# A norm's column sum in another product's stream, an earlier scan, and a state part whose output goes by groups in alternating halves

## The chip, the core and the metric

The kernel runs on one core of a Trainium2 chip. The metric is the device time of one execution in microseconds (us). Engines: TensorE (PE in the profile, its weight loads PEld), VectorE (DVE), ScalarE (ACT), GpSimd (POOL) and SyncE (SP), which issues most transfers.

## The reference, cut to what matters

Two blocks follow one another on 512 tokens of 2048 channels. The change touches the first: the norm of x, the projection by `w_in`, and of its four quarters the one that goes through a state-space mixer.

```python
hn = rmsnorm(h, norm_gain[i])           # x * rsqrt(mean(x*x) + eps) * gain, per token
proj = hn @ w_in[i]                      # (512, 2048) @ (2048, 4096)
pool_in, pool_gate, ssm_in, ssm_gate = four quarters of proj, 1024 channels each
...
# ssm_mixer: 64 groups of 16 channels, 64 complex states each
bu = einsum('blgc,gnc->blgn', u, bb)     # complex
s[t] = ab * s[t-1] + bu[t]               # per group and state, complex
y = Re(einsum('blgn,gcn->blgc', s, c)) + d_skip * u
g = gelu(y)
hg = g @ w_glu
out = hg[..., :1024] * sigmoid(hg[..., 1024:])
```

## The kernel before

**The stream of weights.** All large products run on TensorE in single precision, each operand split into a high and a low part, so that one tile product is three matmuls. Weights come in pieces of two k-tiles (128 rows of the contraction by 512 columns each): SyncE loads a piece (`raw`), ScalarE casts it to the high part (`whi`, L250), VectorE subtracts for the low part (`wlo`, L182). Loads run six pieces ahead, the splitting three. `gemm` (L288 on) does twelve matmuls of 128x512 per k-tile and then calls `tick()`.

**What sets the order.** Everything else on TensorE is put between k-tiles: `side(steps, ticks, least)` (L117) registers a list of steps, and each `tick()` runs the next ones, one per tick or at the rate that `least` and the length give; `None` is an empty step. TensorE's instructions stand in the order in which the program writes them; the order on the other engines is set by a scheduler when the program is built. Temporary tiles come from pools: `t4` with 30 buffers, `t2` with 8, PSUM with five banks for the large products (`mm`) and three for the rest (`aux`).

**The norm of x.** The first two products are linear in x, so x goes in unscaled, and the factor per token is multiplied in afterwards. It comes from the generator `norm_x`: the column sum of the squares (`colsum`, L897: four matmuls into `norm_x`), then `rsq` on VectorE (fourteen small operations, `rsv`, `rsy`, `rst`), then `rows` (L345: four transposes that spread the factor over the partitions) and its copy `r1row`. `put` multiplies a result tile by `r1row` and stores it to `ud` in DRAM. In `blocks` (L1589) the column sum is at tick 13 of the first product, `rsq` behind it at high priority, and `rows` at the first tick of the second product, with the first four `put` behind.

**The state part.** One side list begins with the second product and goes on through the gates' six products. It builds tables (`ssm_tables`, products of 128x1024 named `bb`, `bbt`), then for each half h of the 64 groups and each j of four: `pw` (powers of the transition, 128x1024 on VectorE), `kk` (eight matmuls), two `wb` steps (transposes), `uu` (the load of U from `ud` on SyncE's queue), and `xx` (eight matmuls, whose result ScalarE copies into the states `XS`). After a table `kd` is stored to DRAM, the scan runs on VectorE: 63 recurrences of four small operations each (`sc`, `XS`), three per tick. Then the output: `prep(j, h)` loads T (from `kd`, on GpSimd's queue), computes O (three products), and has ScalarE copy the shifted states into `sx` (L641, two copies); `mm(j, h, g4)` (L653, L654) does eight matmuls with weights of 64 columns and 128 moving columns, into the 64 partitions of PSUM that belong to half h, and ScalarE copies them to `yv`; `fin` transposes and applies the gelu.

**Beside it.** `K.ada(0, 5)` is a second side list with the modulation vector of the second block, spread over the 96 ticks of the gates: loads `wa` on SyncE's queue, products on VectorE (L191) and tiny matmuls `fin` (L946).

Of the kernel before, what the change touches and what calls it, by code (L numbers as in the profile page):

```python
# [16 lines left out]
P = 128  # L17
# [22 lines left out]
class Kernel:  # L40
# [504 lines left out]
    def ssm_in_steps(self, h):  # L545

        nc = self.nc
# [43 lines left out]
        steps = [lambda: pw(0)]  # L591
        for j in range(4):
            steps += [lambda j=j: (kk(j), wb(j, 0)), lambda j=j: wb(j, 1), lambda j=j: uu(j)]
            if j < 3:
                steps.append(lambda j=j: pw(j + 1))
            steps.append(lambda j=j: xx(j))
        if h == 1:
            def kd():
                self.kd = self.dram("kd", [2 * P - 16, 1024])
                z = self.t4("z", [P, 1024])  # L600
                nc.gpsimd.memset(z, 0.0)
                nc.gpsimd.dma_start(self.kd[P:, :], z[:P - 16, :])
                nc.gpsimd.dma_start(self.kd[:P, :], self.ksb.rearrange("p g c -> p (g c)"))
            steps.append(kd)
# [15 lines left out]
    def ssm_out_steps(self):  # L620
# [4 lines left out]
        def init():  # L625
            self.d2 = self.c_table(1)
            st["T"] = [self.t4("T", [P, 8, 8, 16]) for _ in range(2)]

        def prep(j, h):
            gs = slice(h * 32 + j * 8, h * 32 + j * 8 + 8)  # L630
            T = st["T"][h]
            kd = self.kd[:P, gs.start * 16:gs.stop * 16]
# [3 lines left out]
            o = st["o", j, h] = self.t4("O", [P, 8, 8, 16])  # L636
            self.powers(o, 0, gs, self.d1, self.d2)
            sx = st["sx", j, h] = self.t2("sx", [P, 8, 64])
            nc.vector.memset(sx[:, :, 0], 0.0)
            for r in range(2):  # L640
                nc.scalar.copy(sx[r * 64:r * 64 + 64, :, 1:64],  # L641
                               self.XS[h * 64:h * 64 + 64, 0:63, r, j * 8:j * 8 + 8].rearrange("p k g -> p g k"))
            if h == 0:
                st["yv", j] = self.t4("yv", [P, 8, P])

        def mm(j, h, g4):
            hp = slice(h * 64, h * 64 + 64)
            T, o, sx = st["T"][h], st["o", j, h], st["sx", j, h]
            ps = self.aux("mm")
            for gg in range(4):  # L650
                g = g4 * 4 + gg
                out = ps[hp, gg * P:(gg + 1) * P]
                nc.tensor.matmul(out, self.U[j][:, h, g, :], T[:, :, g, :], start=True, stop=False)  # L653
                nc.tensor.matmul(out, sx[:, g, :], o[:, g].rearrange("p i c -> p (i c)"), start=False, stop=True)  # L654
            nc.scalar.copy(st["yv", j][hp, :, g4 * 64:(g4 + 1) * 64].rearrange("p i (g c) -> p g i c", g=4),
                           ps[hp, :].rearrange("p (g i c) -> p g i c", g=4, i=8))
# [16 lines left out]
        steps = [init, lambda: prep(0, 0)]  # L673
        for j in range(4):
            for h in range(2):
                n = 2 * j + h + 1
                if n < 8:
                    steps.append(lambda n=n: prep(n // 2, n % 2))
                steps += [lambda j=j, h=h: mm(j, h, 0), lambda j=j, h=h: mm(j, h, 1)]
            if j > 0:  # L680
                steps += [lambda j=j: fin(j - 1, 0), lambda j=j: fin(j - 1, 1)]
# [907 lines left out]
def blocks(K, a, dbg):  # L1589
# [16 lines left out]
    K.side([None] * 13 + [lambda: next(norm, None)], 14)  # L1606
# [4 lines left out]
    with K.tc.high_priority():  # L1611
        next(norm, None)
    K.finish(s)
    out, halve = K.ssm_out_steps()
    K.side([lambda: next(norm, None)] + [lambda i=i: put(i, first[i], first[i]) for i in range(4)], 5)
    ssm = K.side([None] + K.steps(K.ssm_tables(), 5) + [None] * 4 + K.ssm_in_steps(0) + K.ssm_in_steps(1)
                 + out[:1] + K.ssm_scan_steps() + out[1:], 111)
# [6 lines left out]
    ada = K.side(K.ada(0, 5), 96, 0)  # L1624
# [34 lines left out]
```

## Time and profile before

| | us |
|---|---|
| median of 3 runs (lowest to highest) | 3242.53 (3242.39 to 3245.29) |
| the profiled execution | 3245.36 |
| its span | 3243.6 |
| its mean granted clock of TensorE | 0.991 |

The profile is of one execution. Its span is the time between its first and its last instruction; 1.8 us lie around it. Rows are told by line of the program, engine, operation and tile names (out<-in). A single-precision matmul that isn't split stands in the trace as two records. A row's duration can reach a little over the start of the next row on its engine, since operations are pipelined; where a cost is a share of a sequence it is taken from start to next start. `PEclk` is the clock granted to TensorE, as a share of full speed (2.4 GHz); 0.50 is its lower level, 1.2 GHz.

### The profile page before, as it was taken

The page shows a single profiled execution, that of the slowest core. Times are in us where ns is not written, and L with a number is a line of the kernel's source. Part 1 is how long each engine was busy: PE and PEld are TensorE (multiplying, and loading weights), DVE is VectorE, ACT ScalarE, POOL GpSimd, SP SyncE. Part 2 cuts the span into 40 slices and gives each one's busy share as a digit, 9 for nine tenths or more (in the row PEclk, how much of TensorE's full clock was granted, in tenths as well). Part 3 has the DMA queues.
Part 4 walks back from the last instruction along what each step waited for, and adds up shares of the span by engine and source line. Part 5 has one row for each costly group of instructions (what it writes and reads, how often), then busy time and mean ns, then how long its engine had stood idle before and what let it go on. Part 6 is the DMA issues. An engine that isn't in the chain of part 4 may idle for free.

```text
span 3243.6 us, 50768 instructions
## 1 busy us (share of the span) xinstructions
PE 3161.7 (97%) x18812; PEld 2783.9 (86%) x18812; DVE 2378.8 (73%) x4659; ACT 1332.7 (41%) x2004; POOL 62.1 (2%) x114
## 2 busy tenths in 40 slices
PE   7998999999999999999999899999999999999998
PEld 6887787888899777778779799999999999888887
DVE  8569556876888677776755977888888888864445
ACT  6332453223356454443534553333434334333433
POOL 0000000000000000000000000000000000000000
PEclk9999999999999999999999999999999999999999
DMA  6555444865657444353425563444444444964664
GB/s 193 179 181 188 150 150 152 272 188 166 204 173 256 160 133 153 121 172 121 133 78 169 172 218 104 116 120 118 118 118 118 118 118 146 359 211 154 194 198 160
DMA packets 403865, 531.35 MB, mean 164 GB/s; under 512 B 42544, under 2 KB 225968, under 8 KB 403616
## 3 DMA queue, kind: packets, MB, share of 16 engines
q1 hardware_dynamic: 393408, 503.03, 49.4%
q0 software_dynamic: 5856, 17.11, 1.8%
q10 hardware_dynamic: 4352, 7.96, 0.7%
q8 instruction: 147, 2.41, 0.3%
q14 instruction: 102, 0.84, 0.1%
HBM read 491.34 MB, written 36.63 MB: 163 GB/s over the span
## 4 chain that ended last, share of the span: by engine, by line
PE 86%; DVE 9%; DMA 2%; issue 1%; ACT 1%; SPq 0%; DVEq 0%; ACTq 0%
PE mm L303 37%; PE mm L1390 17%; PE mm L1500 14%; PE p L1390 7%; PE mm L301 5%; DVE wlo L182 2%; PE probs L1070 2%; DMA wa<-in_w_ada_dram 1%; PE mix L1118 1%; DVE sc L182 1%; DVE ada L191 1%; PE turn L1110 1%; PE mm L653 1%; DVE acc L182 0%; PE mm L654 0%
## 5 line engine op out<-in xcount | busy, mean ns | idle before, releaser
L182 DVE TENSOR_TENSOR wlo<-raw,whi 128x1024 fp32r<-128x1024 f32 (+1 forms) x607 | 751.8, 1240 | 508.7 <-ACT whi L250 434.7
L250 ACT CAST whi<-raw 128x1024 fp32r<-128x1024 f32 (+1 forms) x455 | 491.9, 1082 | 890.3 <-PE mm L303 501.4
L303 PE MATMUL mm<-H,whi 128*128 128x512 f32 (+1 forms) x2048 | 514.5, 343 | 2.2 <-ACT pp L863 2.2
L1500 PE MATMUL mm<-whi,u 128*128 128x512 f32 x1344 | 414.7, 390 | 0.0
L303 PEld LDWEIGHTS mm<-H,whi 128*128 128x128 f32 x2048 | 347.9, 191 | 49.3 <-issue 9.8
L303 PE MATMUL mm<-H,wlo 128*128 128x512 f32 (+1 forms) x1024 | 346.2, 338 | 1.5 <-DVE wlo L182 1.5
L303 PE MATMUL mm<-X,whi 128*128 128x512 f32 x1024 | 325.9, 400 | 7.0 <-ACT whi L250 6.6
L268 ACT CAST whi<-raw 128x1024 fp32r<-128x1024 f32 x152 | 159.7, 1051 | 400.8 <-issue 232.4
L303 PE MATMUL mm<-M,whi 128*128 128x256 f32 (+1 forms) x1408 | 312.9, 318 | 4.6 <-ACT u L194 1.9
L1500 PEld LDWEIGHTS mm<-whi,u 128*128 128x128 f32 x1344 | 251.6, 188 | 52.1
L191 DVE SCALAR_TENSOR_TENSOR ada<-wa,siluc,ada 128x512 f32<-128x512 f32 x360 | 269.1, 747 | 36.2 <-DMA wa<-in_w_ada_dram 31.4
L1500 PE MATMUL mm<-wlo,u 128*128 128x512 f32 x672 | 261.5, 389 | 0.0
L303 PEld LDWEIGHTS mm<-M,whi 128*128 128x128 f32 x1408 | 235.3, 194 | 20.9 <-ACT u L194 2.1
L303 PEld LDWEIGHTS mm<-X,whi 128*128 128x128 f32 x1024 | 190.8, 191 | 48.1 <-ACT whi L250 6.6
L1390 PE MATMUL mm<-s,thi 128*128 128x256 f32 x1216 | 232.0, 283 | 0.0
L1390 PE MATMUL mm<-M,whi 128*128 128x256 f32 x1216 | 231.9, 283 | 0.0
L303 PE MATMUL mm<-M,wlo 128*128 128x256 f32 (+1 forms) x704 | 222.3, 316 | 5.0 <-DVE wlo L182 5.0
L303 PEld LDWEIGHTS mm<-H,wlo 128*128 128x128 f32 x1024 | 195.3, 191 | 23.1 <-DVE wlo L182 1.7
L303 PE MATMUL mm<-X,wlo 128*128 128x512 f32 x512 | 202.1, 395 | 0.5 <-DVE wlo L182 0.5
L1390 PEld LDWEIGHTS mm<-M,whi 128*128 128x128 f32 x1216 | 189.8, 192 | 0.1
L1390 PEld LDWEIGHTS mm<-s,thi 128*128 128x128 f32 x1216 | 189.7, 192 | 0.0
L1390 PE MATMUL mm<-M,wlo 128*128 128x256 f32 x608 | 172.1, 283 | 0.0
(377 smaller groups left out, 5806.5 us busy)
## 6 DMA issues: line engine op xcount, KB each, us to landing
wa<-in_w_ada_dram SPq DMA_DIRECT2D x192, 512.0 KB, 6.0
raw<-in_w_in_dram SPq DMA_DIRECT2D x111, 512.0 KB, 3.8
raw<-in_w_down_dram SPq DMA_DIRECT2D x88, 512.0 KB, 4.2
raw<-in_w_out_dram SPq DMA_DIRECT2D x80, 512.0 KB, 3.9
ur<-us SPq DMA_DIRECT2D x140, 256.0 KB, 4.6
raw<-in_w_in_dram SPq DMA_DIRECT2D x130, 256.0 KB, 3.1
raw<-in_w_ple_gate_dram SPq DMA_DIRECT2D x48, 512.0 KB, 3.9
raw<-in_w_gate_dram SPq DMA_DIRECT2D x152, 128.0 KB, 2.1
```

The costliest lines, as they stand in the source:

```text
L182: self.nc.vector.tensor_tensor(o, x, y, op=op)
L191: self.nc.vector.scalar_tensor_tensor(o, x, s, y, op0=op0, op1=op1)
L250: nc.scalar.copy(h, r)
L268: nc.scalar.copy(hv, v)
L301: nc.tensor.matmul(ps[i], x[k][:, xi, c], wt[:, a, :], **fl)
L303: nc.tensor.matmul(ps[i][:, cs], wt[:, a, c], x[k][:, xi, cs], **fl)
L653: nc.tensor.matmul(out, self.U[j][:, h, g, :], T[:, :, g, :], start=True, stop=False)
L1070: nc.tensor.matmul(ps[:, :n], q[:, i * P:n], k[:, :n], start=True, stop=True)
L1110: nc.tensor.transpose(pt[:, b * P:(b + 1) * P], p[:, b * P:(b + 1) * P], self.ident)
L1118: nc.tensor.matmul(po[:, :P], pT[:, b * P:(b + 1) * P], v(b, h), start=(b == 0), stop=(b == i))
L1390: nc.tensor.matmul(ps[j][:, s], wt[:, s, slot], self.C[k][j][xi], start=(k == 0 and s == 0 and i == 0), stop=(k == 7 and s == 1 and i == 2))
L1500: nc.tensor.matmul(ps[b], u[a][:, xi, b * P:(b + 1) * P], wt[:, a, :], start=(n == a == j == 0), stop=(n == NU - 1 and a == 1 and j == 2))
```

## The change

1. The column sum of the norm moves out of the first product into the second, to its second tick; `rsq` follows two ticks later, without high priority; `rows` comes at the seventh tick, and the four `put` at the eighth to eleventh.
2. The load of U is issued in the step of `kk` and the first `wb`; a step per j and half falls away, eight in all. The scan comes eight ticks earlier, and nine empty ticks are put behind it.
3. `kd` is stored by eight transfers, with its columns in the order j, group of four, half, instead of one.
4. The output goes by groups of four with both halves in one tile: `prep(j, g4)` loads a T for it (from the `t4` pool; before there were two fixed T tiles) and computes an O by six products of half the size; the `sx` copies for both halves are made at `g4 == 0`. `mm(j, g4)` does sixteen matmuls, whose halves alternate, into all 128 partitions of PSUM; eight such steps stand in place of sixteen of eight matmuls, and one copy to `yv` in place of two.
5. `K.ada(0, 5)` has 28 empty steps behind its first 24.

```diff
--- before.py
+++ after.py
@@ -590,7 +590,7 @@
 
         steps = [lambda: pw(0)]
         for j in range(4):
-            steps += [lambda j=j: (kk(j), wb(j, 0)), lambda j=j: wb(j, 1), lambda j=j: uu(j)]
+            steps += [lambda j=j: (uu(j), kk(j), wb(j, 0)), lambda j=j: wb(j, 1)]
             if j < 3:
                 steps.append(lambda j=j: pw(j + 1))
             steps.append(lambda j=j: xx(j))
@@ -600,7 +600,12 @@
                 z = self.t4("z", [P, 1024])
                 nc.gpsimd.memset(z, 0.0)
                 nc.gpsimd.dma_start(self.kd[P:, :], z[:P - 16, :])
-                nc.gpsimd.dma_start(self.kd[:P, :], self.ksb.rearrange("p g c -> p (g c)"))
+
+                for n in range(8):
+                    j, g4 = divmod(n, 2)
+                    nc.gpsimd.dma_start(self.kd[:P, n * P:(n + 1) * P].rearrange("p (h n) -> p h n", h=2),
+                                        self.ksb.rearrange("p (h g) c -> p h (g c)", h=2)
+                                        [:, :, (j * 8 + g4 * 4) * 16:(j * 8 + g4 * 4 + 4) * 16])
             steps.append(kd)
         return steps
 
@@ -624,36 +629,42 @@
 
         def init():
             self.d2 = self.c_table(1)
-            st["T"] = [self.t4("T", [P, 8, 8, 16]) for _ in range(2)]
-
-        def prep(j, h):
-            gs = slice(h * 32 + j * 8, h * 32 + j * 8 + 8)
-            T = st["T"][h]
-            kd = self.kd[:P, gs.start * 16:gs.stop * 16]
+
+        def prep(j, g4):
+
+            T = st["T", j, g4] = self.t4("T", [P, 8, 8, 16])
+            n = 2 * j + g4
+            kd = self.kd[:P, n * P:(n + 1) * P]
 
             nc.gpsimd.dma_start(T.rearrange("p i g c -> p i (g c)"),
                                 bass.AP(tensor=kd.tensor, offset=kd.offset, ap=[[1024, P], [16 * 1024, 8], [1, P]]))
-            o = st["o", j, h] = self.t4("O", [P, 8, 8, 16])
-            self.powers(o, 0, gs, self.d1, self.d2)
-            sx = st["sx", j, h] = self.t2("sx", [P, 8, 64])
-            nc.vector.memset(sx[:, :, 0], 0.0)
-            for r in range(2):
-                nc.scalar.copy(sx[r * 64:r * 64 + 64, :, 1:64],
-                               self.XS[h * 64:h * 64 + 64, 0:63, r, j * 8:j * 8 + 8].rearrange("p k g -> p g k"))
-            if h == 0:
+            o = st["o", j, g4] = self.t4("O", [P, 2, 4, 8, 16])
+            for h in range(2):
+                g0 = h * 32 + j * 8 + g4 * 4
+                self.powers(o[:, h], 0, slice(g0, g0 + 4), self.d1, self.d2)
+            if g4 == 0:
                 st["yv", j] = self.t4("yv", [P, 8, P])
-
-        def mm(j, h, g4):
-            hp = slice(h * 64, h * 64 + 64)
-            T, o, sx = st["T"][h], st["o", j, h], st["sx", j, h]
+                for h in range(2):
+                    sx = st["sx", j, h] = self.t2("sx", [P, 8, 64])
+                    nc.vector.memset(sx[:, :, 0], 0.0)
+                    for r in range(2):
+                        nc.scalar.copy(sx[r * 64:r * 64 + 64, :, 1:64],
+                                       self.XS[h * 64:h * 64 + 64, 0:63, r, j * 8:j * 8 + 8].rearrange("p k g -> p g k"))
+
+        def mm(j, g4):
+            T, o = st.pop(("T", j, g4)), st.pop(("o", j, g4))
             ps = self.aux("mm")
             for gg in range(4):
                 g = g4 * 4 + gg
-                out = ps[hp, gg * P:(gg + 1) * P]
-                nc.tensor.matmul(out, self.U[j][:, h, g, :], T[:, :, g, :], start=True, stop=False)
-                nc.tensor.matmul(out, sx[:, g, :], o[:, g].rearrange("p i c -> p (i c)"), start=False, stop=True)
-            nc.scalar.copy(st["yv", j][hp, :, g4 * 64:(g4 + 1) * 64].rearrange("p i (g c) -> p g i c", g=4),
-                           ps[hp, :].rearrange("p (g i c) -> p g i c", g=4, i=8))
+
+                out = [ps[h * 64:h * 64 + 64, gg * P:(gg + 1) * P] for h in range(2)]
+                for h in range(2):
+                    nc.tensor.matmul(out[h], self.U[j][:, h, g, :], T[:, :, h * 4 + gg, :], start=True, stop=False)
+                for h in range(2):
+                    nc.tensor.matmul(out[h], st["sx", j, h][:, g, :], o[:, h, gg].rearrange("p i c -> p (i c)"),
+                                     start=False, stop=True)
+            nc.scalar.copy(st["yv", j][:, :, g4 * 64:(g4 + 1) * 64].rearrange("p i (g c) -> p g i c", g=4),
+                           ps.rearrange("p (g i c) -> p g i c", g=4, i=8))
 
         def fin(j, s2):
             if s2 == 0:
@@ -670,15 +681,13 @@
             self.g[f] = self.pair("g")
             self.split(self.g[f], st["gt", f % 4][:, f // 4])
 
-        steps = [init, lambda: prep(0, 0)]
-        for j in range(4):
-            for h in range(2):
-                n = 2 * j + h + 1
-                if n < 8:
-                    steps.append(lambda n=n: prep(n // 2, n % 2))
-                steps += [lambda j=j, h=h: mm(j, h, 0), lambda j=j, h=h: mm(j, h, 1)]
-            if j > 0:
-                steps += [lambda j=j: fin(j - 1, 0), lambda j=j: fin(j - 1, 1)]
+        steps = [init, lambda: prep(0, 0), lambda: prep(0, 1)]
+        for n in range(8):
+            if n < 6:
+                steps.append(lambda n=n: prep(n // 2 + 1, n % 2))
+            steps.append(lambda n=n: mm(n // 2, n % 2))
+            if n % 2 and n > 2:
+                steps += [lambda j=n // 2: fin(j - 1, 0), lambda j=n // 2: fin(j - 1, 1)]
         return steps + [lambda: fin(3, 0), lambda: fin(3, 1)], [lambda f=f: halve(f) for f in range(8)]
 
 
@@ -1603,25 +1612,25 @@
 
     norm = K.norm_x()
     s = K.side([None] * 5 + K.steps(K.ssm_scalars(), 7), 16)
-    K.side([None] * 13 + [lambda: next(norm, None)], 14)
     ps = K.gemm(K.X, hook=lambda k: K.scale_x(k + 4) if k + 4 < KT else None)
     first = [K.t2("u") for _ in range(4)]
     for i in range(4):
         K.nc.scalar.copy(first[i], ps[i])
-    with K.tc.high_priority():
-        next(norm, None)
     K.finish(s)
     out, halve = K.ssm_out_steps()
-    K.side([lambda: next(norm, None)] + [lambda i=i: put(i, first[i], first[i]) for i in range(4)], 5)
+    n1 = lambda: next(norm, None)
+    K.side([None, n1, None, n1, None, None, n1] + [lambda i=i: put(i, first[i], first[i]) for i in range(4)], 11)
     ssm = K.side([None] + K.steps(K.ssm_tables(), 5) + [None] * 4 + K.ssm_in_steps(0) + K.ssm_in_steps(1)
-                 + out[:1] + K.ssm_scan_steps() + out[1:], 111)
+                 + out[:1] + K.ssm_scan_steps() + [None] * 9 + out[1:], 108)
     ps = K.gemm(K.X)
     for i in range(4):
         put(4 + i, K.t2("u"), ps[i])
     K.pin, K.pgate, K.sgate = (K.dram(n, [1024, S]) for n in ("pin", "pgate", "sgate"))
     K.ada_setup()
     K.ada = K.ada_steps()
-    ada = K.side(K.ada(0, 5), 96, 0)
+
+    ada = K.ada(0, 5)
+    ada = K.side(ada[:24] + [None] * 28 + ada[24:], 96, 0)
     K.gates(0, K.pin)
     K.gates(1, K.pgate)
     K.gates(2, K.sgate)
```

The scheduler sets how this comes out on the engines beside TensorE. First VectorE's order around the end of the reciprocal root (`rsy`, `rst`), before. `bb` and `bbt` are the tables' products, `u` the result tiles that `put` scales:

```order
L182 TENSOR_TENSOR bbt_701<-b_118_673,ssq_481 128x1024
L188 TENSOR_SCALAR rst_614<-rst_614 128x4
L182 TENSOR_TENSOR wlo_636<-raw_457,whi_635 128x1024
L182 TENSOR_TENSOR rsy_613<-rsy_613,rst_614 128x4
L182 TENSOR_TENSOR bb_122_699<-bb_122_699,bbt_701 128x1024
L346 COPY r1row_651<-rows_652 128x512
```

and after, from the middle of the root on (`pw` and `pwt` are the powers for the first j, `d` a table of c):

```order
L182 TENSOR_TENSOR rst_692<-rsy_691 128x4
L186 TENSOR_SCALAR d_727<-d_727 64x1024
L182 TENSOR_TENSOR rst_692<-rst_692,rsv_689 128x4
L182 TENSOR_TENSOR pwt_840<-acc_82_448,bb_118_672 128x1024
L188 TENSOR_SCALAR rst_692<-rst_692 128x4
L182 TENSOR_TENSOR pw_839<-pw_839,pwt_840 128x1024
L182 TENSOR_TENSOR rsy_691<-rsy_691,rst_692 128x4
L182 TENSOR_TENSOR wlo_712<-raw_568,whi_711 128x1024
L182 TENSOR_TENSOR rst_692<-rsy_691 128x4
L182 TENSOR_TENSOR rst_692<-rst_692,rsv_689 128x4
```

Before, the root ended ahead of the tables' second half (`bb_123`); after, all products of the tables, a whole `pw` and two more pieces' `wlo` stand ahead of its end.

Second, ScalarE's order at the end of the scan (`sx` waits for the last states), before:

```order
L250 CAST whi_2592<-raw_2379 128x1024
L250 CAST whi_2662<-raw_2449 128x1024
L250 CAST whi_2729<-raw_2520 128x1024
L250 CAST whi_2783<-raw_2590 128x1024
L641 COPY sx_2718<-XS 64x8x63 x2
L641 COPY sx_2751<-XS 64x8x63 x2
L641 COPY sx_2827<-XS 64x8x63 x2
L655 COPY yv_2722<-mm_2767 64x4x8x16
```

and after:

```order
L250 CAST whi_2563<-raw_2361 128x1024
L250 CAST whi_2593<-raw_2427 128x1024
L651 COPY sx_2711<-XS 64x8x63 x2
L250 CAST whi_2623<-raw_2513 128x1024
L651 COPY sx_2715<-XS 64x8x63 x2
L651 COPY sx_2772<-XS 64x8x63 x2
L651 COPY sx_2776<-XS 64x8x63 x2
L250 CAST whi_2653<-raw_2561 128x1024
L250 CAST whi_2683<-raw_2591 128x1024
```

Before, no cast stood between the first six `sx` copies; after, one stands behind the first pair, and the next ones behind six more copies.

Third, SyncE's queue around the loads of U, before:

```order
L224 DMA raw_1150<-in_w_in_dram 128x2x512
L919 DMA wa_1146<-in_w_ada_dram 128x2x512
L578 DMA U_1186<-ud_163 128x512
L919 DMA wa_1188<-in_w_ada_dram 128x2x512
L224 DMA raw_1192<-in_w_in_dram 128x2x512
L919 DMA wa_1238<-in_w_ada_dram 128x2x512
L578 DMA U_1186<-ud_167 128x512
L224 DMA raw_1242<-in_w_in_dram 128x2x512
```

and after:

```order
L928 DMA wa_1083<-in_w_ada_dram 128x2x512
L578 DMA U_1099<-ud_163 128x512
L224 DMA raw_1122<-in_w_in_dram 128x2x512
L928 DMA wa_1118<-in_w_ada_dram 128x2x512
L928 DMA wa_1146<-in_w_ada_dram 128x2x512
L224 DMA raw_1171<-in_w_in_dram 128x2x512
L928 DMA wa_1167<-in_w_ada_dram 128x2x512
L578 DMA U_1212<-ud_164 128x512
```

`ud_163` is the third j of half 0, `ud_164` the fourth, `ud_167` the third of half 1. Loads of U stand between loads of weights and of `wa` in both, directly behind a `wa` at some places.

## Rows read from the trace of the kernel before

**Rows 1.** Page, part 1: busy time of each engine, share of the span, instructions.
```profile
PE 3161.7 (97%) x18812; PEld 2783.9 (86%) x18812; DVE 2378.8 (73%) x4659; ACT 1332.7 (41%) x2004; POOL 62.1 (2%) x114
```

**Rows 2.** TensorE's waits: line <- releaser: us in total, times, longest.
```profile
PE mm L654 <- ACT sx L641: 14.3, 1, 14.3
...
PE rows L345 <- DVE rsy L182: 8.8, 1, 8.8
...
PE norm_x L897 <- DVE acc L182: 1.8, 1, 1.8
```

**Rows 3.** Stretches: us, PE, PEld, DVE, ACT, POOL busy, PEclk, DMA share, GB/s.
```profile
50.00:100.00 50.00, 40.78 (x174) 33.60 (x175) 39.54 (x75) 18.04 (x12) 1.78 (x1) 0.90 0.50 137
...
300.00:350.00 50.00, 35.73 (x176) 29.03 (x175) 39.16 (x131) 13.92 (x16) 1.15 (x2) 0.83 0.29 90
```

**Rows 4.** VectorE's timeline: start, us, operation, ended wait in brackets.
```profile
52.19 1.95 DVE L182 TENSOR_TENSOR wlo<-raw,whi 128x1024 fp32r<-128x1024 f32 x1
...
56.84 1.22 DVE L182 TENSOR_TENSOR bb<-b,ssq 128x1024 f32<-128x1024 f32 x1
...
57.97 0.16 DVE L182 TENSOR_TENSOR rst<-rsy 128x4 f32<-128x4 f32 x1
...
61.13 1.44 DVE L182 TENSOR_TENSOR rst<-rsy 128x4 f32<-128x4 f32 x1
...
79.20 0.69 DVE L182 TENSOR_TENSOR u<-u,r1row 128x512 f32<-128x512 f32 x1
```

**Rows 5.** GpSimd's timeline in the same stretch.
```profile
60.81 1.78 POOL L522 TENSOR_SCALAR_AFFINE_SELECT ksb<-ksb 128x1024 f32<-128x1024 f32 x1 [58.51 <-DVE sstmp L182]
```

**Rows 6.** TensorE's timeline, the broadcast of the norm.
```profile
68.54 1.09 PE L345 MATMUL rows<-ident,rsy 128*128 128x128 f32 x4 [8.80 <-DVE rsy L182]
```

**Rows 7.** Stretches (columns of rows 3) behind the two long waits.
```profile
68.50:74.00 5.50, 5.46 (x16) 4.48 (x17) 4.65 (x6) 0.00 (x0) 0.00 (x0) 0.52 0.84 218
328.30:333.00 4.70, 4.63 (x18) 4.01 (x19) 3.56 (x4) 4.60 (x6) 0.00 (x0) 0.50 0.25 68
```

**Rows 8.** TensorE's timeline, first three steps of output matmuls and around.
```profile
328.37 0.69 PE L654 MATMUL mm<-O,sx 128*64 128x128 f32 x2 [14.27 <-ACT sx L641]
...
333.82 0.62 PE L303 MATMUL mm<-X,whi 128*128 128x512 f32 x2
...
335.56 0.38 PE L654 MATMUL mm<-O,sx 128*64 128x128 f32 x2
...
336.88 0.38 PE L654 MATMUL mm<-O,sx 128*64 128x128 f32 x2
...
338.68 0.62 PE L303 MATMUL mm<-X,whi 128*128 128x512 f32 x2
...
341.41 0.61 PE L303 MATMUL mm<-X,whi 128*128 128x512 f32 x2
...
342.86 0.43 PE L653 MATMUL mm<-T,U 128*64 128x128 f32 x2
...
347.69 0.43 PE L653 MATMUL mm<-T,U 128*64 128x128 f32 x2
```

**Rows 9.** TensorE's timeline, the last `xx` ahead of the scan.
```profile
239.61 1.89 PE L584 MATMUL xx<-U,wb 128*128 128x64 f32 x16
```

**Rows 10.** VectorE's timeline, the scan's first operation.
```profile
243.90 0.22 DVE L182 TENSOR_TENSOR sc<-XS,a8i 128x64 f32<-128x64 f32 x1
```

**Rows 11.** ScalarE's timeline, the `sx` copies behind the scan.
```profile
326.20 6.48 ACT L641 COPY sx<-XS 64x504 f32<-64x504 f32 x6 [11.61 <-DVE XS L182]
```

**Rows 12.** One stretch, the scan: us, PE, PEld, DVE busy with `ada` alone, ...
```profile
243.90:326.20 82.30, 0.23 (x2) 0.14 (x2) 15.99 (x22) 0.94 0.57 182
```

**Rows 13.** TensorE's timeline, a small narrow product and the next matmul.
```profile
274.18 0.23 PE L946 MATMUL fin<-ada,quads 128*32 128x16 f32 x2
274.34 0.73 PE L303 MATMUL mm<-X,whi 128*128 128x512 f32 x2
```

**Rows 14.** DMA issues: queue, operation, count, KB each, median us to landing.
```profile
U<-ud SPq DMA_DIRECT2D x8, 256.0 KB, 5.0
```

## The prediction

> **What bounds the kernel now.** I read the page first. TensorE is busy for 97% of the span [rows 1], so the weight stream on TensorE is the bound nearly everywhere, and a change gains where TensorE stands still, runs at the lower clock, or spends time on small matmuls. The list of TensorE's waits comes next [rows 2]: the longest single one, 14.27 us, is the first output matmul of the state part waiting for ScalarE's copy `sx` of the scanned states; 8.80 us is the broadcast `rows` of the norm waiting for VectorE's `rsy`; 1.8 us is the norm's column sum. All three lie on lines that the change moves. The table of stretches shows the rest [rows 3]: TensorE is 40.8 of 50 us busy from 50 to 100 and 35.7 of 50 from 300 to 350, the two places of these waits. So there is at most 10.6 + 14.3 us of standing still to be had, plus what the clock loses after each idle time, plus the cost of the 128 small output matmuls.
>
> **Norm.** What holds `rows` is VectorE. From 52.19 on it works without a gap through three `wlo` (1.95 us, of which the last 0.08 lie under the next operation: 1.87 [rows 4]), two 128x1024 products of the tables (1.13 from start to next start, 56.84 to 57.97 [rows 4]), small operations, the chain of fourteen operations of the reciprocal root, and one of these that is drawn out to 1.44 us [rows 4] while a GpSimd operation runs [rows 5]. Then `rows` starts, at 68.54 [rows 6], with VectorE's last `rsy`. After the change `rows` stands behind six more k-tiles of the second product, but the order shows that VectorE now puts two more `wlo`, seven more 128x1024 products (rest of the tables, the first `pw`) and one more half-height operation ahead of the last `rsy`: 2 x 1.87 + 7 x 1.13 + 0.7 = 12.4 us, so `rows` starts at about 68.5 + 12.4 = 80.9. TensorE reached `rows` at 68.54 - 8.80 = 59.74 [rows 6]; without the wait of 1.8 for the column sum and with six k-tiles of 2.73 (338.68 to 341.41 [rows 8]) more it would come there at 74.3. So a wait of some 6.5 us remains, part of it perhaps as short waits for `wlo`. Before, `rows` started at 68.54 with six k-tiles fewer done; that is 84.9 on the same count; now it is 80.9: **4.0 us gained**. Its bounds are 0 (the chain grows by as much as the tiles that now stand ahead) and 13.2 (both waits gone, 10.6, and the 2.6 us that the clock of 0.52 costs in the 5.5 us behind it [rows 7]). I take the 4.0, since VectorE has no idle time there in which the chain could be quicker; the cold stretch after the wait stays.
>
> **Scan against its consumer.** From the last `xx` [rows 9] to the first output matmul TensorE had 26 ticks (one tick is one k-tile), 71 us; with eight ticks fewer ahead of the scan and nine empty ones behind it, it has 36, that is 36 x 2.73 = 98 us. The scan starts 2.4 us after `xx` and takes 82.3 (243.90 to 326.20 [rows 10, 11]). In that time VectorE also did 22 operations of `ada`, 16.0 us [rows 12]; by the order two are left in it, since the 28 empty steps of that list fall there: -14.5. Added by the order are four 128x512 products of the gates at 0.61 (0.69 less the same 0.08 [rows 4]), 2.4, and 18 such products for `O` instead of 6 of 1.13, 4.2. So the scan ends 2.4 + 82.3 - 14.5 + 6.6 = 76.8 us after `xx`, and the first pair of `sx` copies (1.08 each: six in 6.48 [rows 11]) is through at 79, 19 us ahead of the matmul. **The 14.3 us go whole.** What is late next: `sx` copies wait on ScalarE ahead of the `whi` casts of two pieces of weights. By the order a pair stands ahead of one cast and six more copies ahead of the next; those pieces are needed some 87 and 92.5 us after `xx`, and would be ready (copies, a cast of about a copy's length, a subtraction of 1.9) at 82 and 90. Cover is 5 and 2.5 us; if it is missed, I put the loss at 4 us at most. I take 0.
>
> **The clock after that wait.** Behind it the granted clock was 0.50 for 4.7 us [rows 7]. The rest of that step and the three half-groups of the k-tile after it took 5.45 us (328.37 to 333.82 [rows 8]), and the same instructions of the next step 3.12 (335.56 to 338.68): **2.3 us gained**, with the wait.
>
> **Half as many steps.** A step of eight small matmuls between two k-tiles costs, from 342.86 to 347.69 [rows 8], 4.83 us. One k-tile is 2.73, and eight matmuls at 0.22 each (335.56 to 336.88 are six) are 1.76; 0.34 is left for going over to the small matmuls and back. Sixteen steps become eight: **2.7 us gained**; bounds 0 and 2.9. The copies out of PSUM halve in number and take no TensorE time.
>
> **Halves in turns.** Each of these matmuls uses 64 of 128 columns of the array, and takes 0.22 us as two records of 0.11. Before, neighbours wrote the same 64 partitions of PSUM; now neighbours alternate between the lower and the upper 64. No row of before shows two such matmuls next to each other. From below: no effect, 0 (a loss has no reason, as the number of matmuls, their sizes and the weights they load are the same). From above: two at a time, half of 128 x 0.22 = 28.2, so 14.1 us. Between them I go by narrow rows. With full-width weights even half as many columns need 0.12 a record (16 records of `xx` in 1.89 [rows 9]), so there it isn't the columns but the load of weights, or what goes with it, that sets the pace; two small records with 32 columns of weights stand 0.16 us ahead of the next matmul (274.18 and 274.34 [rows 13]), 0.08 each. That is the nearest row in width; at 0.08 instead of 0.11 the 256 records give **7.7 us**.
>
> **At no cost.** The U loads come three ticks (8.2 us) ahead of their use instead of two; they land in 5.0 [rows 14]. The table `kd` is stored in eight parts on GpSimd's queue, during the scan, where nobody waits for it. The `ada` list has the same steps, faster before and after its pause, on the same engines.
>
> **Sum.** 4.0 + 14.3 + 2.3 + 2.7 + 7.7 = 31.0 us. The profiled execution's span of 3243.6 becomes 3212.6 and its time of 3245.36 becomes 3214.4; the runs' median lies 2.8 below that execution, and 3242.5 - 31.0 gives 3211.5: I say **3212**.
>
> **Rivals.** (1) *Halves fully side by side.* If the alternating matmuls run two at a time, the last term is 14.1 and the time 3205. For it: their weights and outputs use different column halves. Against it: the 0.08 of the narrow records, which have hardly any columns to stream and are no quicker. The Trainium skill, "TensorE: Matmul & The Clock Gate", Part 3 (packing small matmuls), says that matmuls whose outputs lie in different column groups run concurrently, with 2.38 times measured for three; but also that weight loads overlap running matmuls only where the row group differs, and here both halves use all rows. No run here shows either yet. (2) *Halves not side by side.* The records stay 0.11 apart, the term is 0: 3219. For it: each small matmul has its own weights to load, and all rows here with their own weights are 0.08 or slower. (3) *The norm moves nothing, or all of it.* If VectorE's chain grows by the whole 16 us, 3216; if TensorE no longer waits, 3202. (4) *The cover on ScalarE is missed*: short waits for `whi` in the scan, 3216, and 3223 together with (2). (5) *Slower.* SyncE issues the U loads from the same queue as the weights and the `wa` of `ada`, in order; a `wa` that waits for a free buffer holds what stands behind it. In both orders a `wa` stands directly ahead of two of the U loads; after, the `ada` list runs at 0.84 steps per tick there instead of 0.55. If each of eight `xx` waited 4 us or more, all 31 us would be gone: over 3243. It decides at a U that lands more than 12 us after its slot (three ticks and 4 us), against the 5.0 of the row; no `xx` waits now. (6) *The change doesn't do what it says*, which would need the scan to end more than 20 us later than I reckon, so that most of the wait stays: about 3228.
>
> **Chances.** Forecast (halves partly side by side, between 3208 and 3215) 0.36; rival 1 with what goes with it 0.26; rival 2 0.24; rival 4 on top of a smaller gain 0.05; rival 6 0.04; rival 5 0.05. The range: from 3202 (1 with a better norm) to 3226 (2 with losses on ScalarE). A difference of 0.2% (6.5 us) is about what a measurement of this kernel tells from none. Only rival 5, and small parts of 6, lie above 3236: faster 0.89, same 0.06, slower 0.05.
>
> **What would show it.** In the profile after: no wait of the output matmul for `sx`, and a granted clock of 1.00 through that stretch; a `rows` that starts near 81 with a wait of about 6.5 us ahead of it and a low clock behind; eight steps of sixteen small matmuls, each with a spacing of 0.11 (rival 2), 0.08 (forecast) or 0.055 (rival 1) per record; no waits of `xx` for U, none of `mm` for `whi` over 1 us in the scan. The forecast falls if a new wait above 5 us stands there, or if the steps of output matmuls cost as much as before.

## The result and the profile after

The changed kernel takes 3208.77 us (median of 4 runs, 3208.1 to 3209.4), the kernel before beside it 3243.91 (median of 4). The ratio is 0.989, with a 95% interval of 0.9875 to 0.9905: 35.1 us less. The forecast was 3212, 31.0 us less.

The first line is from the page of the kernel after (busy time of each engine), the next ones are from TensorE's waits (line <- releaser: us in total, times, longest).

```profile
PE 3143.2 (98%) x18812; PEld 2767.5 (86%) x18812; DVE 2379.6 (74%) x4683; ACT 1328.6 (41%) x1996; POOL 67.1 (2%) x121
```

```profile
PE rows L345 <- DVE rsy L182: 5.4, 1, 5.4
...
PE mm L303 <- DVE gt L182: 1.3, 1, 1.3
...
PE mm L303 <- DVE XS L182: 0.4, 1, 0.4
```

Against [rows 2], the wait of an output matmul for `sx` is not in the list at all, nor is that of the column sum; `rows` waits 5.4 us instead of 8.8. Two short waits of the gates' products stand in the scan, for VectorE's `gt` and `XS`. TensorE is busy 18.5 us less than before [rows 1] with as many instructions, so about half of the gain was never a wait. The stretches of [rows 3], after (us, PE, PEld, DVE, ACT, POOL busy, PEclk, DMA share, GB/s):

```profile
50.00:100.00 50.00, 42.87 (x196) 34.87 (x196) 40.64 (x78) 19.04 (x14) 1.51 (x1) 0.97 0.57 158
...
300.00:350.00 50.00, 50.00 (x317) 40.72 (x316) 30.46 (x51) 29.70 (x33) 3.03 (x4) 1.00 0.59 184
```

The second hole is closed, busy 50.00 of 50 at full clock; the first is only 2 us smaller. TensorE's timeline of one output step after, and the start of the step behind it:

```profile
324.92 0.44 PE L662 MATMUL mm<-T,U 128*64 128x128 f32 x4
325.19 0.39 PE L664 MATMUL mm<-O,sx 128*64 128x128 f32 x4
325.41 0.39 PE L662 MATMUL mm<-T,U 128*64 128x128 f32 x4
325.63 0.39 PE L664 MATMUL mm<-O,sx 128*64 128x128 f32 x4
...
326.50 0.39 PE L664 MATMUL mm<-O,sx 128*64 128x128 f32 x4
326.82 0.73 PE L303 MATMUL mm<-X,whi 128*128 128x512 f32 x2
...
332.48 0.44 PE L662 MATMUL mm<-T,U 128*64 128x128 f32 x4
```

Each row now holds four records (a matmul of either half) where the rows of before held two, and the next row starts 0.22 us later as before [rows 8]: two matmuls in the time of one. The whole step of sixteen takes 1.90 us (324.92 to 326.82); before, a step of eight took 1.89 (from 342.86 [rows 8] to this row):

```profile
344.75 0.73 PE L303 MATMUL mm<-X,whi 128*128 128x512 f32 x2
```

How far the first block got shows where `glu`'s product starts, the first product behind all that the change touches. The row of before, then that of after:

```profile
466.71 0.61 PE L303 MATMUL mm<-g,whi 128*128 128x512 f32 x2
```

```profile
431.72 0.62 PE L303 MATMUL mm<-g,whi 128*128 128x512 f32 x2
```

35.0 us earlier: the whole gain is made by then. This start is used below beside the times, since it holds nothing of the stretches that the edits don't touch.

### The profile page after: what moved, and what is told of

Read it like the earlier page. It is cut to its first block, busy times and chain, and to the rows that moved or that the text cites. A ratio compares the mean times of both kernels' runs of the same rounds, so it can differ in the third digit from the quotient of the medians.

```text
span 3207.7 us, 50820 instructions
## 1 busy us (share of the span) xinstructions
PE 3143.2 (98%) x18812; PEld 2767.5 (86%) x18812; DVE 2379.6 (74%) x4683; ACT 1328.6 (41%) x1996; POOL 67.1 (2%) x121
## 4 chain that ended last, share of the span: by engine, by line
PE 86%; DVE 9%; DMA 3%; issue 1%; ACT 1%; SPq 0%; DVEq 0%; ACTq 0%
PE mm L303 37%; PE mm L1399 17%; PE mm L1509 14%; PE p L1399 7%; PE mm L301 5%; DVE wlo L182 2%; PE probs L1079 2%; PE mix L1127 1%; DMA wa<-in_w_ada_dram 1%; DVE sc L182 1%; PE turn L1119 1%; DVE acc L182 1%; PE xx L584 0%; PE kk L562 0%; ACT whi L250 0%
```

## The experiments

The first seven edits start from the kernel after, the eighth from the one with the broadcast later, the last three put one part of the change into the kernel before.

| kernel | median us | `glu` starts at |
|---|---|---|
| before | 3243.91 | 466.71 |
| after | 3208.77 | 431.72 |
| halves apart | 3223.47 | 443.53 |
| runs of two | 3210.59 | 432.41 |
| sixteen steps | 3217.64 | 438.93 |
| norm as before | 3213.32 | 434.25 |
| broadcast later | 3203.57 | 425.10 |
| no empty steps | 3219.93 | 442.94 |
| no pause of `ada` | 3216.94 | 439.02 |
| four steps | 3213.96 | 433.52 |
| output alone | 3234.30 | 453.75 |
| scan alone | 3234.07 | 452.27 |
| norm alone | 3241.04 | 462.09 |

**Halves apart.**

```diff
-            for gg in range(4):
-                g = g4 * 4 + gg
...
-                for h in range(2):
-                    nc.tensor.matmul(out[h], self.U[j][:, h, g, :], T[:, :, h * 4 + gg, :], start=True, stop=False)
-                for h in range(2):
-                    nc.tensor.matmul(out[h], st["sx", j, h][:, g, :], o[:, h, gg].rearrange("p i c -> p (i c)"),
+            for h in range(2):
+                for gg in range(4):
+                    g = g4 * 4 + gg
...
+                    nc.tensor.matmul(out, self.U[j][:, h, g, :], T[:, :, h * 4 + gg, :], start=True, stop=False)
+                    nc.tensor.matmul(out, st["sx", j, h][:, g, :], o[:, h, gg].rearrange("p i c -> p (i c)"),
...
```

> The changed kernel with its eight steps of sixteen small matmuls, but within a step first all eight of the lower half, then all eight of the upper. Theory (the halves run side by side when neighbours differ in half; the number of steps is worth only 0.3 us a step): records of one half stand 0.11 us apart again, a step of sixteen costs about 3.5 us instead of 1.75, less one overlap at the border between the halves (0.2 us). Eight steps: 12 to 14 us more, 3221 to 3223 us. Rival (the gain came from fewer and wider steps or tiles, not from the turns): within 2 us of the changed kernel, 3207 to 3211 us.

Measured 3223.47 (3221.21 to 3224.95): 0.5 above the theory's range and far from the rival's. TensorE's timeline of a step, at the border between the halves and its end:

```profile
336.14 0.43 PE L661 MATMUL mm<-T,U 128*64 128x128 f32 x2
...
337.28 0.38 PE L662 MATMUL mm<-O,sx 128*64 128x128 f32 x2
337.50 0.44 PE L661 MATMUL mm<-T,U 128*64 128x128 f32 x4
337.72 0.44 PE L662 MATMUL mm<-O,sx 128*64 128x128 f32 x4
338.00 0.38 PE L661 MATMUL mm<-T,U 128*64 128x128 f32 x2
...
339.40 0.73 PE L303 MATMUL mm<-X,whi 128*128 128x512 f32 x2
```

Two records per row again, except at the border, where two rows hold four: the last two matmuls of the lower half (T, O) and the first two of the upper (T, O) run side by side. These are two overlaps, where one was expected, so sixteen matmuls take 14 slots of 0.22 us. The step takes 3.26 us (336.14 to 339.40) instead of 1.90; 8 x 1.36 = 10.9 us, and the start of `glu` moves by 11.8, of which 0.9 were there before the first output step. With the two overlaps counted (8 x 0.44 = 3.5 us, an estimate from the spacing) the turns are worth 14.4 us by this kernel. So the turns are what brings two matmuls side by side; groups, wide tiles and fewer copies alone don't.

**Runs of two.**

```diff
             for gg in range(4):
...
                 for h in range(2):
-                    nc.tensor.matmul(out[h], self.U[j][:, h, g, :], T[:, :, h * 4 + gg, :], start=True, stop=False)
-                for h in range(2):
-                    nc.tensor.matmul(out[h], st["sx", j, h][:, g, :], o[:, h, gg].rearrange("p i c -> p (i c)"),
+                    g = g4 * 4 + gg
...
+                    nc.tensor.matmul(out, self.U[j][:, h, g, :], T[:, :, h * 4 + gg, :], start=True, stop=False)
+                    nc.tensor.matmul(out, st["sx", j, h][:, g, :], o[:, h, gg].rearrange("p i c -> p (i c)"),
...
```

> The changed kernel, but the halves alternate by two matmuls (both of the lower half's group, T then O, then both of the upper) instead of by one. Theory A (a matmul may start beside the one ahead of it if that lies in the other half, and waits for it if it lies in the same half): every second neighbour pair is of two halves, but each matmul still has one of the other half beside it, so sixteen take 8.5 to 9 slots of 0.22 us instead of 8: 1 to 2 us more in eight steps, 3209.5 to 3211 us. Theory B (only two that stand directly in turns, started as a pair, run together; behind a same-half neighbour nothing overlaps): half or none of the overlap is left, 7 to 14 us more, 3216 to 3223 us.

Measured 3210.59, `glu` 0.7 us later: the time of theory A. A step of it:

```profile
332.86 0.45 PE L661 MATMUL mm<-T,U 128*64 128x128 f32 x4
333.13 0.40 PE L662 MATMUL mm<-O,sx 128*64 128x128 f32 x4
...
334.44 0.44 PE L662 MATMUL mm<-O,sx 128*64 128x128 f32 x4
334.81 0.73 PE L303 MATMUL mm<-X,whi 128*128 128x512 f32 x2
```

1.95 us (332.86 to 334.81), 0.05 more than with strict turns. Theory A's picture holds only in part: by it, the upper half's first T would start beside the lower half's O, 0.27 us behind the lower T. The first row shows four records of T, so the two T start together, and the two O behind them. The upper T has started ahead of the lower O, which stands before it in the program. At the border in the kernel with the halves apart it is the same: there, too, the upper half's T starts with the lower half's last T and ahead of its last O. The halves ran as two streams, each in its own order; both kernels show a matmul pass one of the other half, and no run shows one pass two.

**Sixteen steps.**

```diff
-            for gg in range(4):
+            for gg in range(2 * q, 2 * q + 2):
...
-            steps.append(lambda n=n: mm(n // 2, n % 2))
+            steps += [lambda n=n: mm(n // 2, n % 2, 0), lambda n=n: mm(n // 2, n % 2, 1)]
```

> The changed kernel with halves in turns, but each group's sixteen matmuls in two steps of eight at two ticks, so that the number of steps is sixteen as before. Theory: only the price of going over to small matmuls and back, 0.34 us by the rows of before, eight times: 2 to 3.5 us more, 3211 to 3212 us. Rival (the steps themselves were the larger part of the gain): 8 us more or beyond, over 3216 us.

Measured 3217.64, 8.9 more than after: beyond the theory's figure and in the rival's range. The trace splits it, and the rival's reason isn't in it. A step of eight starts 3.97 to 4.01 us ahead of the next row behind one k-tile:

```profile
329.87 0.44 PE L664 MATMUL mm<-T,U 128*64 128x128 f32 x4
...
330.90 0.74 PE L303 MATMUL mm<-X,whi 128*128 128x512 f32 x2
...
333.88 0.44 PE L664 MATMUL mm<-T,U 128*64 128x128 f32 x4
```

With a k-tile of 2.73 a step costs 1.24 to 1.28; sixteen are 20 to 20.5 us, against 8 x 2.10 = 16.8 after (324.92 to 332.48 is 7.56, less two k-tiles): 3.0 to 3.7 us for the steps, as expected. The rest is something that the edit brought with it; a part shows in its waits:

```profile
PE mm L303 <- DVE gt L182: 3.3, 5, 1.5
```

2.0 us more than after of gates' products that wait for VectorE. Of the 7.2 us at `glu`, 0.8 were there before the first output step (it starts at 317.78 instead of 316.97); what is left, about 1, I did not find. So the edit is no clean measure of the steps; the timeline is.

**Norm as before.**

```diff
+    K.side([None] * 13 + [lambda: next(norm, None)], 14)
     ps = K.gemm(K.X, hook=lambda k: K.scale_x(k + 4) if k + 4 < KT else None)
...
+    with K.tc.high_priority():
+        next(norm, None)
...
-    K.side([None, n1, None, n1, None, None, n1] + [lambda i=i: put(i, first[i], first[i]) for i in range(4)], 11)
+    K.side([lambda: next(norm, None)] + [lambda i=i: put(i, first[i], first[i]) for i in range(4)], 5)
```

> The changed kernel with the norm's column sum, root and broadcast at their places of before. Theory (the norm part is worth the 4 us of the sum): the waits of 1.8 and 8.8 us and 5 us at the lower clock are back, 5.4 us of wait and two of 0.9 and 0.8 for wlo go: 3 to 4.5 us more, 3212 to 3213 us. Rival (later work takes the gain up again, since VectorE is the engine that is late there): within 1 us, 3208 to 3210 us.

Measured 3213.32 (3211.07 to 3218.38), `glu` 2.5 us later. The waits of this kernel:

```profile
PE rows L345 <- DVE rsy L182: 7.3, 1, 7.3
...
PE norm_x L906 <- DVE acc L182: 1.3, 1, 1.3
```

They are 2 us shorter than in the profile of before [rows 2]; the two other kernels with this norm (output alone, scan alone) show 7.2 and 7.1 us for `rows`, so [rows 2] has a rather dear one. The move is worth 2.5 us by the trace and 4.5 by the medians, around the theory's figure; not zero.

**Broadcast later.**

```diff
-    K.side([None, n1, None, n1, None, None, n1] + [lambda i=i: put(i, first[i], first[i]) for i in range(4)], 11)
+    K.side([None, n1, None, n1, None, None, None, None, n1] + [lambda i=i: put(i, first[i], first[i]) for i in range(4)], 13)
```

> The changed kernel with the norm's broadcast two ticks later (ninth tick of the second product instead of the seventh), and the four puts behind it as well. Theory (the 5.4 us wait is VectorE's chain alone, whose end does not depend on where the broadcast stands): TensorE does 5.4 us of matmuls in that time, the wait falls to under 1 us, and with it the stretch at the lower clock (about 1 us): 3202 to 3204 us. Rival (the puts, and the loads of U that wait for them, are then late, or VectorE takes up two more pieces of weights first): a wait of xx or of the broadcast takes the gain back, 3207 to 3211 us.

Measured 3203.57 (3202.80 to 3205.08; ratio to before 0.988, interval 0.9866 to 0.9893), as the theory has it: 5.2 less than after, 6.6 at `glu`, and faster than both kernels. The broadcast in TensorE's timeline, and the stretch:

```profile
82.50 0.60 PE L345 MATMUL rows<-ident,rsy 128*128 128x128 f32 x4
```

```profile
50.00:100.00 50.00, 47.65 (x226) 38.71 (x225) 44.52 (x80) 20.44 (x16) 2.30 (x1) 1.00 0.60 169
```

No wait, and it starts at nearly the time of after (82.12): VectorE's chain ends when it ends, and two more k-tiles fit ahead of it. The lower clock is gone with the wait. `xx` has no wait for U.

**No empty steps, and no pause.**

```diff
-                 + out[:1] + K.ssm_scan_steps() + [None] * 9 + out[1:], 108)
+                 + out[:1] + K.ssm_scan_steps() + out[1:], 99)
```

> The changed kernel without the nine empty steps behind the scan. Theory: the output matmuls then come nine k-tiles (24.5 us) earlier, at about 292.5 in the profile, and the scan's last states with four copies sx are through at about 301: a wait of 7 to 10 us and 1 to 2 us at the lower clock are back, 3217 to 3221 us. Rival (eight ticks fewer ahead of the scan and the pause of ada are enough): within 2 us of the changed kernel.

```diff
-    ada = K.side(ada[:24] + [None] * 28 + ada[24:], 96, 0)
+    ada = K.side(ada, 96, 0)
```

> The changed kernel without the 28 empty steps in the ada list, so that by the order VectorE has 30 more of its operations among the scan's (0.66 us each, 20 us). Theory: the scan ends 18 to 20 us later, at about 316, its copies at about 320, the output matmul at 317 waits 3 to 5 us, with 1 to 2 us at the lower clock: 3212 to 3216 us. Rival (VectorE has room in the scan, since the recurrences depend on each other and leave gaps that ada fills): within 1.5 us of the changed kernel.

Measured 3219.93 without the empty steps (`glu` 11.2 later), in its theory's range, and 3216.94 without the pause (7.3 later), 0.9 above its theory's range. The wait is back in both; first the row without empty steps, then that without the pause:

```profile
PE mm L664 <- ACT sx L651: 6.8, 2, 5.4
```

```profile
PE mm L664 <- ACT sx L651: 4.2, 2, 2.5
```

Both parts are needed. ScalarE's `sx` copies without the pause start at 318.24, against 296.15 in the kernel after:

```profile
318.24 2.09 ACT L651 COPY sx<-XS 64x504 f32<-64x504 f32 x2 [5.32 <-DVE XS L182]
```

```profile
296.15 2.21 ACT L651 COPY sx<-XS 64x504 f32<-64x504 f32 x2 [5.44 <-DVE XS L182]
```

22 us for 30 more operations of `ada` and what goes with them: VectorE is busy for 75.10 of the scan's 77.91 us in the kernel after (218.24 to 296.15), so the scan leaves no gaps that others could fill for nothing.

**Four steps.** With the broadcast later, and the output matmuls of a j in one step.

```diff
-        steps = [init, lambda: prep(0, 0), lambda: prep(0, 1)]
+        steps = [init, lambda: prep(0, 0), lambda: prep(0, 1), lambda: prep(1, 0)]
         for n in range(8):
-            if n < 6:
-                steps.append(lambda n=n: prep(n // 2 + 1, n % 2))
-            steps.append(lambda n=n: mm(n // 2, n % 2))
+            if n < 5:
+                steps.append(lambda n=n: prep((n + 3) // 2, (n + 3) % 2))
+            if n % 2:
+                steps.append(lambda j=n // 2: (mm(j, 0), mm(j, 1)))
```

> The changed kernel with the broadcast of the norm two ticks later and the output matmuls of a j in one step: four steps of 32 small matmuls instead of eight of sixteen. Theory: four goings-over to small matmuls and back fewer, 0.35 us each: 1 to 1.5 us less than with the later broadcast alone, 3202 to 3203 us. Rival (two banks of PSUM taken at once and their copies delay the steps behind): 3204 us or more.

Measured 3213.96, 10.4 more than with the broadcast later alone: the rival's time, with another reason. Waits of this kernel:

```profile
PE fin L675 <- ACT yv L666: 5.3, 1, 5.3
PE mm L303 <- DVE gt L182: 4.1, 3, 3.0
```

8 us of the 10.4 are these two, counting 2.7 of the second (with the broadcast later alone, `gt` is waited for 1.4). The transpose `fin` waits for ScalarE's copies to `yv`. The trace names VectorE's `O` as their releaser and not the banks of PSUM, and VectorE stood still for 3.42 us ahead of that `O`, until a load of `wa` for a product of `ada` had landed:

```profile
344.27 0.75 DVE L191 SCALAR_TENSOR_TENSOR ada<-wa,siluc,ada 128x512 f32<-128x512 f32 x1 [3.42 <-DMA wa<-in_w_ada_dram]
344.94 0.68 DVE L182 TENSOR_TENSOR O<-O,pwt 128x512 f32<-128x512 f32 x1
...
345.66 1.07 ACT L666 COPY yv<-mm 128x512 f32<-128x512 f32 x2 [7.02 <-DVE O L182]
```

Ahead of the longest wait for `gt` VectorE does nine products for `O` in a row (317.40 to 322.82). What the wider step saves is far less: its 32 matmuls take 3.64 us, two steps of sixteen 3.80.

**The parts alone.** The diff's hunks for the output and `kd`; for `uu`, the empty steps and `ada`; and for the norm, each put into the kernel before.

> The kernel before with the output part of the change alone (groups with both halves in one tile, eight steps in turns, the table kd in eight parts); norm, scan inputs, gap and ada as before. Theory (the parts are separate; this one is worth 16.9 us of TensorE time, but asks more of what comes just before): eight steps of 2.1 us instead of sixteen of 2.25 save some 17 to 19 us; the scan has 4 us more of the products for O among it and the first step needs four copies sx instead of two, so the wait of 14.3 us becomes 17 to 20: 3228 to 3232 us. Rival (the gain of the turns appears only together with the earlier scan): 3238 us or more.

> The kernel before with the scan's part of the change alone (U loaded in the step of kk, nine empty steps behind the scan, the pause of ada). Theory: the wait of 14.3 us and 2.3 us at the lower clock go, nothing else changes: 3225 to 3228 us. Rival (waits for weights behind the copies on ScalarE, or for U, take some of it): 3229 to 3236 us.

> The kernel before with the norm's part of the change alone. Theory: 3 to 4.5 us less as in the sum, 3238 to 3240 us, unless the loads of U come too late behind the later puts (a wait of xx of several us then stands in the trace, and the time is 3243 or more).

Measured 3234.30, 3234.07 and 3241.04. These runs scattered more than the others (the kernel before, 15 runs beside them, 3238.83 to 3249.37, median 3243.95), so I read the traces: `glu` starts 13.0, 14.4 and 4.6 us earlier than before (466.71 less the table's starts). TensorE's wait for `sx` in the first of them is, as expected, longer than before:

```profile
PE mm L664 <- ACT sx L651: 17.1, 2, 15.7
```

The parts' sum is 32.0 of 35.0; the 2.8 us more of this wait, which the earlier scan takes away in the whole change, are the difference. By the medians the sum is only 9.7 + 9.9 + 2.9 = 22.5, and all three come out slower than their theories said, the scan alone in its rival's range. That rival's waits for `whi` or U are not in its trace; 2.2 us of waiting for `gt` are. Of the gain at `glu`, 1.7 us of the scan's and 2.9 of the norm's are lost again later in the profiles, where nothing was changed (below): their spans are 3230.9 and 3241.9 us, that of before 3243.6. The rest lies in the scatter of the runs; I can't assign it.

## Why the prediction was right

The time is right, one of the five terms is not: the halves ran wholly side by side, which was rival 1 (chance 0.26) and not the forecast (0.36). That 3208.77 still lies between 3208 and 3215, the band given for halves partly side by side, is luck. Rival 1's own 3205 was missed by 3.8 us: 1.4 are short waits in the scan that the sum had at nothing, 1.4 the kernel before, which ran slower beside this one than in the runs that the sum started from (3243.91 instead of 3242.53), and about 1 is open.

**Norm, 4.0.** `rows` was to start at 80.9 after a wait of 6.5; it starts at 82.12 after 5.43, behind two waits of 0.9 and 0.8 for `wlo`:

```profile
67.61 0.50 PE L303 MATMUL mm<-X,wlo 128*128 128x512 f32 x1 [0.94 <-DVE wlo L182]
...
74.12 0.50 PE L303 MATMUL mm<-X,wlo 128*128 128x512 f32 x1 [0.77 <-DVE wlo L182]
...
82.12 1.08 PE L345 MATMUL rows<-ident,rsy 128*128 128x128 f32 x4 [5.43 <-DVE rsy L182]
```

That is 2.8 by the count of the prediction; about 1 us comes from a shorter stretch at the lower clock, which the prediction had left unchanged. From there to the last `xx` nothing moves: it starts 25.5 us earlier than [rows 9], and 21.8 of these are the eight ticks; 3.7 remain for the norm:

```profile
214.07 1.89 PE L584 MATMUL xx<-U,wb 128*128 128x64 f32 x16
```

Alone it is 2.5 to 4.6. VectorE's chain as the thing that holds `rows` is shown by the later broadcast; that I did not see there that two ticks more would be free is the 5 us left on the table.

**Scan, 14.3 and 2.3.** Both are gone, as the stretch from 300 to 350 shows. The scan's states are there 80.2 us after the end of the last `xx` (215.96 to 296.15) instead of 76.8, mostly because the gates' products among it take more than reckoned (eight in 7.2 us; before, four in 2.7), and the first matmul comes at 316.97, 20.8 later. The cover that the sum counted on is real on ScalarE's side: no wait for `whi` stands there. On VectorE's side it costs 1.4 us more than before in gates' products that wait for `gt` and `XS`; the sum had taken these at nothing.

**Steps, 2.7.** 3.0 to 3.7 by the spacing of the sixteen-step kernel.

**Halves, 7.7.** This is the term that was mis-sized. Steps and halves together went from 16 x 2.10 to 8 x 2.10, that is 16.8 us instead of 10.4; with the steps at 3.0 to 3.7, the turns are worth 13 to 14: all of the upper bound of 14.1, rival 1. The failing step is the choice of the narrow row: 0.08 a record in [rows 13] is two records that stand alone between large matmuls, with going over and back in it, and the 0.12 of `xx` belongs to weights of full width. Neither says what two half-width streams cost each other. Sixteen matmuls in turns in the time of eight (1.90 and 1.89 us) show that they cost nothing, and the kernel with the halves apart that it is the turns.

The Trainium skill, "TensorE: Matmul & The Clock Gate", Part 3, says that matmuls whose outputs lie in different column groups run concurrently. The trace agrees: 1.90 us for sixteen, 3.26 with the halves apart. The same part of the Trainium skill says that weight loads overlap running matmuls only where the row group differs, which the prediction weighed against rival 1. It does not show as a cost here: both halves use all rows, and sixteen matmuls with sixteen sets of weights still take the time of eight.

**The sum.** 3.7 + 14.3 + 2.3 + 16.8 - 1.4 = 35.7, against 35.0 at `glu` and 35.1 of the medians. The slower rival has no trace: no `xx` waits, in any of the kernels.

## What to carry to other kernels

Matmuls that use half of the array's columns should alternate between the halves, singly or in runs of two: here it halved their time (0.22 to 0.11 us each), once both halves' operands were at hand in the same step. A wait on an engine's chain is not shortened by moving the consumer a little: read when the chain ends, and put the consumer behind that, as long as what follows it has room. Where an edit is worth some us in three thousand, read its effect at the first instruction behind the part that it touches, and not from the end alone.

## What had not been expected of the hardware

Half-width matmuls overlap at the border of two runs, too, and two pairs there: the first matmul of the second run starts together with the last but one of the first run, ahead of the last one, which stands before it in the program (337.50 and 337.72 in the kernel with the halves apart). So the order in the program decides how many overlap, and no pairing has to be marked in it.

Stretches that no edit touches differ by some us. From the column sum of a later norm to the first attention product it is 181.4 us in the kernel after and 184.8 with the halves apart, with the same instructions; rows of after, then of the halves apart:

```profile
881.08 1.02 PE L906 MATMUL norm<-ones,acc 128*128 128x1 f32 x8 [1.31 <-DVE acc L182]
...
1062.49 1.14 PE L1079 MATMUL probs<-qk,qk 64*128 64x128 f32 x6
```

```profile
891.49 1.02 PE L904 MATMUL norm<-ones,acc 128*128 128x1 f32 x8 [1.31 <-DVE acc L182]
...
1076.25 1.14 PE L1077 MATMUL probs<-qk,qk 64*128 64x128 f32 x6
```

Of the 3.4 us, some 1.4 are the granted clock behind the same wait of 1.31 us (0.02 of 70 us), which fell to its lower level for a while in one and not in the other (stretches of after, then of the halves apart; the clock is the third figure from the end):

```profile
881.00:951.00 70.00, 69.06 (x576) 68.92 (x577) 63.78 (x147) 40.68 (x68) 0.00 (x0) 1.00 0.55 168
```

```profile
891.50:961.50 70.00, 69.15 (x564) 68.97 (x565) 62.35 (x143) 39.60 (x66) 0.00 (x0) 0.98 0.53 166
```

Another 1.2 us is a wait that only the kernel with the halves apart has there:

```profile
1015.64 0.39 PE L303 MATMUL mm<-H,wlo 128*128 128x256 f32 x1 [1.25 <-DVE wlo L182]
```

Why the one clock fell and the other did not, no run shows. Behind the wait for the norm the clock of the changed kernel was back sooner: 0.50, then 0.73, then 1.00 from 86 on, within 4 us of the wait, against 5.5 us at 0.52 before [rows 7]:

```profile
82.10:84.00 1.90, 1.88 (x7) 1.71 (x8) 1.90 (x2) 0.00 (x0) 0.00 (x0) 0.50 0.74 251
84.00:86.00 2.00, 2.00 (x8) 1.58 (x7) 1.97 (x4) 0.00 (x0) 0.00 (x0) 0.73 0.42 97
```
